# First adaLN columns in groups of 128, the first in-projection weights as single chunks, fewer adaLN tiles on TensorE, gates spread through DRAM, and eight FFN groups in two turns

## Chip, cores and metric

The kernel runs on one core of a Trainium2 chip. The metric is the device time of one execution in microseconds (us), the median of several runs on the chip. The engines are TensorE (PE: matmuls; PEld: its weight loads), VectorE (DVE), ScalarE (ACT), GpSimd (POOL) and SyncE (SP), which issues most DMAs.

## The reference

One decoder block in float32, with 256 tokens of width 2048. A vector c gives six rows of 2048 (shift, scale and gate of two sub-layers) by a product with a 2048 x 12288 matrix, which with 100 MB is the largest tensor. What is computed:

```python
mod = silu(c) @ w_ada + b_ada
sh1, sc1, g1, sh2, sc2, g2 = split(mod, 6)

h = modulate(rms_norm(x, norm1_g), sh1, sc1)        # h * (1 + sc1) + sh1
q, k, v, gb, gc, xt = split(h @ w_in)               # six parts of 1024 columns
attn = moba_attention(rms_norm(q), rms_norm(k), v)  # 8 heads, 256 tokens: one block, causal
conv = gb * causal_dwconv(gc * xt, conv_w, conv_b)  # 3 taps
mixed = concat(rms_norm(attn, attn_out_g), rms_norm(conv, conv_out_g))
x = x + g1 * (mixed @ w_out)

h2 = modulate(rms_norm(x, norm2_g), sh2, sc2)
u = causal_dwconv(h2 @ w_ffn_up, ffn_conv_w, ffn_conv_b)
u_gate, u_up = split(u)                             # 5632 columns each
x = x + g2 * ((silu(u_gate) * u_up) @ w_ffn_down)
```

## The kernel before

**Precision.** Every large product is done in fp32r, in three parts: a weight tile `raw` is split by ScalarE into `hi` (L230, fp32r) and by VectorE into `lo = raw - hi` (L236); the activations are split in the same way. `mm_tok` issues hi·hi, lo·hi and hi·lo (L380, L381, L382) for each chunk of 128 rows and each half of the tokens. In the FFN's first product (called z in the trace) a wide matmul (L673) has both parts of the activations as 512 moving columns, and a low one (L677) multiplies `lo` with 256.

**Slots.** The weight tiles, mostly of 1 MB, form a list of 204 slots in the order in which TensorE works on them: in-projection, out-projection, then the FFN in 22 groups of 256 columns of gate and up, in four segments, each followed by its part of the down-projection. Five `raw` buffers are filled by SyncE in the order in which they will be used; `hi` and `lo` are made two slots ahead (`LA`). All other work is made of small tasks, which tables in `CFG` place at a slot and, within it, before or after the slot's splits. The order of instructions on each engine is written out by this list; no scheduler changes it.

**In-projection.** Its 12 blocks of 512 columns (`q0`, `q1`, `k0` and so on) come in `turns`, each over a range of the 16 chunks of rows, first two chunks of a pair of blocks, later eight of one. Between turns the sums leave PSUM for SBUF (`evac_in`: ScalarE copies `pa_*` at L391, or VectorE adds at L393).

**The adaLN product.** The class `Ada` works on groups of columns, tile by tile (1 MB each). Some groups are done on TensorE with 32 copies of silu(c) as weights (`crep`), four chunks side by side in the array (L286); the others on VectorE, as a product-and-add with a scalar for each partition (L290, L292). A group on TensorE is copied out by `evac` (L303). `cols` turns scale and shift from a row into columns: transposes on TensorE (L319), then a VectorE reduction (L321) or ScalarE copies with a sum (L326). `spread` gives gates to all partitions by a product with 128 columns of ones (L343) and a copy (L344). The first groups hold scale and shift of two chunks, 256 columns each, with two tiles each.

**The start.** x is loaded, normed, and transposed chunk pair by chunk pair (`xn`, L1037, copied at L1040); with the first columns of scale and shift `h_chunks` (L742 to L749) makes the first two chunks of h, and the main loop begins.

**FFN.** The second norm (`norm2`, L541 to L552) makes chunks 0 to 7 of h2 first, and the first four groups (`split`) are multiplied with chunks 0 to 7, then with 8 to 15; the first half's sums wait in SBUF (`up_sum`: ScalarE L587, VectorE L590, and L595 to add both halves). x1, the result of the first sub-layer, stays in SBUF, and its transposes (L496) are made around the end of the out-projection. PSUM's eight banks are one ring (`bank`).

## Time and profile before

| | us |
|---|---|
| median of 3 runs | 1197.08 |
| lowest and highest run | 1196.53, 1200.62 |
| span of the profiled execution | 1195.2 |

The span is the time from the first to the last instruction of one execution under the profiler, and all rows of the trace are measured from its start. The profiled execution has no time of its own beside the span; the median of the runs stands 1.9 us above it.

In rows of the timeline the columns are the start in us, the duration in us, the engine and the line, the operation, output and inputs (partitions x elements), how many instructions the row joins (x), and in brackets the idle time before it and what ended it. The page lists busy time, share of the span and instructions of each engine; a row of the groups gives the total busy time and the mean of one in ns, and the idle time behind the bar. A row of the waits gives the total us, how often, and the longest. `raw`, `hi` and `lo` are the weight tiles, `ada` an adaLN sum, `adac` its columns, `adab` a gate's broadcast, `m` with a letter an in-projection sum, `pa` with a letter that sum in SBUF.

### The profile page before, as it was taken

The page shows a single profiled execution, that of the slowest core. Times are in us where ns is not written, and L with a number is a line of the kernel's source. Part 1 is how long each engine was busy: PE and PEld are TensorE (multiplying, and loading weights), DVE is VectorE, ACT ScalarE, POOL GpSimd, SP SyncE. Part 2 cuts the span into 40 slices and gives each one's busy share as a digit, 9 for nine tenths or more (in the row PEclk, how much of TensorE's full clock was granted, in tenths as well). Part 3 has the DMA queues.
Part 4 walks back from the last instruction along what each step waited for, and adds up shares of the span by engine and source line. Part 5 has one row for each costly group of instructions (what it writes and reads, how often), then busy time and mean ns, then how long its engine had stood idle before and what let it go on. Part 6 is the DMA issues. An engine that isn't in the chain of part 4 may idle for free.

```text
span 1195.2 us, 15484 instructions
## 1 busy us (share of the span) xinstructions
PE 1169.1 (98%) x6041; PEld 962.5 (81%) x6041; DVE 917.4 (77%) x1099; ACT 614.1 (51%) x850; POOL 1.6 (0%) x9
## 2 busy tenths in 40 slices
PE   5999999999999999999999999999999999999998
PEld 3667788877778778888888888888888888888886
DVE  3889989997888988788787587776745667567676
ACT  5654356555766456565645334545434455344452
POOL 0000000000000000000000000000000000000000
PEclk9999999999999999999999999999999999999999
DMA  9999997998869998755777789654565554674543
GB/s 366 357 409 381 369 378 271 386 348 334 293 234 407 345 370 286 240 183 167 247 255 259 263 302 368 210 181 154 186 229 171 197 181 150 217 235 154 175 136 106
DMA packets 194925, 313.78 MB, mean 263 GB/s; under 512 B 6650, under 2 KB 105500, under 8 KB 194596
## 3 DMA queue, kind: packets, MB, share of 16 engines
q1 hardware_dynamic: 194160, 312.52, 74.1%
q8 instruction: 47, 0.77, 0.2%
q10 hardware_dynamic: 692, 0.28, 0.1%
q14 instruction: 26, 0.21, 0.1%
HBM read 310.67 MB, written 2.10 MB: 262 GB/s over the span
## 4 chain that ended last, share of the span: by engine, by line
PE 93%; DVE 3%; DMA 3%; ACT 1%; issue 0%; SPq 0%; ACTq 0%
PE z L673 27%; PE z L677 14%; DMA raw<-in_w_ada_dram 3%; PE ada L286 2%; PE mc L380 1%; PE mc L381 1%; PE mc L382 1%; PE mx L380 1%; PE mq L380 1%; PE mv L382 1%; PE mg L380 1%; PE mk L380 1%; PE mg L382 1%; PE mx L382 1%; PE mg L381 1%; PE mx L381 1%
## 5 line engine op out<-in xcount | busy, mean ns | idle before, releaser
L236 DVE TENSOR_TENSOR lo<-raw,hi 128x2048 fp32r<-128x2048 f32 (+2 forms) x204 | 448.8, 2206 | 167.2 <-ACT hi L230 158.2
L230 ACT ACTIVATE hi<-raw 128x2048 fp32r<-128x2048 f32 (+2 forms) x204 | 375.9, 1848 | 367.2 <-PE z L673 104.5
L673 PE MATMUL z<-h,hi 128*128 128x512 f32 x1408 | 381.3, 395 | 1.1 <-DVE h L573 1.1
L673 PEld LDWEIGHTS z<-h,hi 128*128 128x128 f32 x1408 | 242.2, 189 | 36.7 <-DVE h L573 2.0
L677 PEld LDWEIGHTS z<-h,lo 128*128 128x128 f32 x1408 | 212.6, 189 | 27.8
L677 PE MATMUL z<-h,lo 128*128 128x256 f32 x1408 | 220.3, 281 | 0.0
L292 DVE SCALAR_TENSOR_TENSOR ada<-raw,csil,ada 128x1024 f32<-128x1024 f32 (+2 forms) x165 | 159.5, 968 | 5.8 <-DMA raw<-in_w_ada_dram 1.8
L590 DVE TENSOR_TENSOR ub<-z,ub 128x256 f32<-128x256 f32 x104 | 37.5, 418 | 33.0 <-ACT ub L587 32.8
L604 ACT ACTIVATE uy<-ub,fc,fc 128x256 f32<-128x256 f32 x88 | 45.7, 591 | 5.5 <-DVE uy L611 5.5
L286 PE MATMUL ada<-raw,crep 128*32 128x512 f32 (+1 forms) x320 | 36.5, 566 | 10.2 <-DMA raw<-in_w_ada_dram 10.2
L611 DVE SCALAR_TENSOR_TENSOR uy<-ub,fc,uy 128x254 f32<-128x254 f32 x88 | 42.5, 483 | 3.1
L620 ACT ACTIVATE gh<-uy 128x512 fp32r<-128x512 f32 x22 | 13.9, 632 | 58.1 <-DVE uy L618 58.1
L609 DVE SCALAR_TENSOR_TENSOR uy<-ub,fc,uy 128x255 f32<-128x255 f32 x88 | 42.1, 479 | 1.5 <-ACT uy L604 1.5
L587 ACT ACTIVATE ub<-z 128x256 f32<-128x256 f32 x104 | 32.2, 382 | 11.6 <-PE z L673 11.6
L614 ACT ACTIVATE uy<-uy 128x512 f32<-128x512 f32 x22 | 13.9, 631 | 39.1 <-DVE uy L611 39.1
L286 PEld LDWEIGHTS ada<-raw,crep 128*32 128x32 f32 x320 | 8.4, 113 | 26.4 <-issue 14.3
L621 DVE TENSOR_TENSOR gl<-uy,gh 128x512 fp32r<-128x512 f32 x22 | 15.2, 693 | 15.4 <-ACT gh L620 15.4
L382 PE MATMUL mv<-hi,h 128*128 128x512 f32 x64 | 25.0, 391 | 1.4 <-DVE h L749 1.4
L380 PE MATMUL mc<-hi,h 128*128 128x512 f32 x64 | 26.2, 409 | 0.0
L380 PE MATMUL mk<-hi,h 128*128 128x512 f32 x64 | 25.3, 396 | 0.7 <-ACT h L746 0.7
L380 PE MATMUL mx<-hi,h 128*128 128x512 f32 x64 | 25.8, 402 | 0.0
L380 PE MATMUL mg<-hi,h 128*128 128x512 f32 x64 | 25.5, 398 | 0.0
(541 smaller groups left out, 1854.3 us busy)
## 6 DMA issues: line engine op xcount, KB each, us to landing
raw<-in_w_ada_dram SPq DMA_DIRECT2D x96, 1024.0 KB
raw<-in_w_ffn_up_dram SPq DMA_DIRECT2D x176, 512.0 KB
raw<-in_w_in_dram SPq DMA_DIRECT2D x48, 1024.0 KB
raw<-in_w_ffn_down_dram SPq DMA_DIRECT2D x24, 1024.0 KB
raw<-in_w_ffn_down_dram SPq DMA_DIRECT2D x24, 768.0 KB
raw<-in_w_out_dram SPq DMA_DIRECT2D x16, 1024.0 KB
xr<-in_x_dram SPq DMA_DIRECT2D x2, 1024.0 KB
x<-in_x_dram SPq DMA_DIRECT2D x8, 256.0 KB
```

Of the source, the lines that this page charges most:

```text
L230: act(hi[:, :nk], t[:, :nk], AF.Copy)
L236: V.tensor_tensor(out=lo[:, :nk], in0=t[:, :nk], in1=hi[:, :nk].bitcast(F32), op=ALU.subtract)
L286: mm(self.acc[q:q + 32, :], crep[:, i, :], t[:, j, :], start=(r == 0 and j < 4), stop=(r == self.tiles - 1 and j >= self.rows - 4), tile_p ...
L292: V.scalar_tensor_tensor(out=self.acc, in0=t[:, j, :], scalar=csil[:, i:i + 1], in1=self.acc, op0=ALU.mult, op1=ALU.add)
L380: mm(o, a, hi[:, k], start=(first and k == 0), stop=False)
L382: mm(o, b, hi[:, k], start=False, stop=(last and k == nk - 1))
L590: V.tensor_tensor(out=d, in0=zp[grp][ft][:, :256], in1=d, op=ALU.add)
L604: act(y, b, AF.Identity, bias=fcols[3][:, i:i + 1], scale=fcols[2][:, i:i + 1])
L609: V.scalar_tensor_tensor(out=y[:, 1:], in0=b[:, :255], scalar=fcols[1][:, i:i + 1], in1=y[:, 1:], op0=ALU.mult, op1=ALU.add)
L611: V.scalar_tensor_tensor(out=y[:, 2:], in0=b[:, :254], scalar=fcols[0][:, i:i + 1], in1=y[:, 2:], op0=ALU.mult, op1=ALU.add)
L673: mm(zp[grp][ft], hi[:, j, ft * P:(ft + 1) * P], h2T[k + j], start=k + j == ks[0], stop=k + j == ks[1] - 1)
L677: mm(zp[grp][ft][:, :256], lo[:, j, ft * P:(ft + 1) * P], h2T[k + j][:, :256], start=False, stop=False)
```

## The change

- **First adaLN groups.** Instead of two groups of 256 columns there are four of 128. The first scale and shift (SC_0, SH_0) are done "directly": each weight chunk is the stationary operand and silu(c) the one moving column (16 products each), so that the result stands in a column at once. SC_1 and SH_1 are done as before, but 128 columns wide. Rows of these tiles are 512 bytes long in DRAM.
- **The first weight slots.** The first turn takes three blocks (q0, q1, k0) for chunk 0 alone, the second the same blocks for chunk 1: 768 KB each, loaded and split in three pieces. There are 205 slots.
- **Tiles on TensorE.** 28 rather than 34, and the four tiles of the first groups; VectorE does 8,192 columns rather than 7,936. VectorE's steps are no longer issued when their tile is due, but in numbers given by tables (`pre`, `carry`).
- **Columns.** `cols` has products with one moving column (62 instructions) in place of 64 transposes and of what followed these.
- **Gates.** `spread` makes 32 copies with two products side by side, VectorE adds the bias, ScalarE's queue sends the row to DRAM and later loads it back to all partitions (`broadcast`).
- **FFN.** Eight groups are worked on in two turns. The wide and the low products of a slot are 16 and 16 instead of 4 and 4 by turns. x1 is parked in DRAM and loaded back.
- **Banks.** Each PSUM bank is held (`keep`) and freed (`drop`) by name. A table `move` shifts tasks by slots.

The diff, cut:

```diff
-CFG = {'ada': [[3, 12, 512, False, 51, 12], [3, 0, 512, True, 58, 2], [2, 0, 1024, False, 24, 17],
...
+CFG = {'ada': [[1, 2, 256, True, 1, 4], [0, 2, 256, True, 1, 1], [1, 4, 512, True, 3, 7], [0, 4, 512, False, 2, 7],
...
- 'turns': [['k', 0, 2], ['c', 0, 2], ['g', 0, 2], ['x', 0, 2], ['v', 0, 2], ['q', 0, 2], ['v', 2, 4], ['x', 2, 4],
...
+ 'turns': [['q0', 3, 0, 1], ['q0', 3, 1, 2], ['c0', 2, 0, 2], ['k1', 1, 0, 2], ['g0', 2, 0, 2], ['v0', 2, 0, 2],
...
+ 'pre': {0: 3,
...
+ 'carry': {0: 2,
...
+ 'move': {'att_n 2': (0, 3),
...
- 'split': [4, 8],
+ 'split': [8, 8],
...
-        return ps.tile([P, 512], F32, tag="b", bufs=8, name=name)
+    now, free, live = [0], list(range(8)), {}
+
+    def bank(name, keep=False):
+        i = next(j for j in free if j not in live.values())
+        free.remove(i)
+        free.append(i)
+        t = ps.tile([P, 512], F32, tag=f"b{i}", bufs=1, name=name)
+        if keep:
+            live[id(t)] = i
+        return t
...
+            self.seen += 1
             for j in range(self.rows):
                 i = self.rows * r + j
-                if self.pe:
+                if self.direct:
+                    mm(self.full[:, 0:1], t[:, j, :], csil[:, i:i + 1], start=i == 0, stop=i == NK - 1)
+                elif self.pe:
                     q = 32 * (j % 4)
...
-                elif i == 0:
-                    V.tensor_scalar(self.acc, t[:, j, :], csil[:, i:i + 1], None, op0=ALU.mult)
                 else:
-                    V.scalar_tensor_tensor(out=self.acc, in0=t[:, j, :], scalar=csil[:, i:i + 1],
-                                           in1=self.acc, op0=ALU.mult, op1=ALU.add)
-            load_next()
+                    later.setdefault(self, []).append((t[:, j, :], i, j == self.rows - 1))
...
-                for k in range(n):
-                    nc.tensor.transpose(p[:, k * P:(k + 1) * P], self.acc[:, (h + k) * P:(h + k + 1) * P], ident)
...
+            for k in range(0 if self.direct else m):
+                mm(p[:, k:k + 1], self.acc[:, k * P:(k + 1) * P], (c32 if self.pe else ones)[:, 0:1],
+                   start=True, stop=True)
+            z = p[:, :m]
...
-                mm(p, c32 if self.pe else ones, a, start=True, stop=True)
-                act(a, p, AF.Copy)
-                gB[self.part, self.c0 // 4 + i // 512] = a
...
+            for q in range(a, a + n):
+                mm(p[32 * q:32 * q + 32, :], ones[:, :32], self.acc[:, (q - a) * 512:(q - a + 1) * 512],
+                   start=True, stop=True, tile_position=(0, 32 * q))
...
+                nc.scalar.dma_start(rowsG[self.part, q], gsum[self.part][32 * q:32 * q + 1, :])
...
+        nc.scalar.dma_start(gB[part, f], rowsG[part, f].partition_broadcast(P))
...
+    def park(f):
+        assert f"ev{f}" in done
+        for t in range(2):
+            parked[t, f] = dram.tile([P, 512], F32, name=f"pk{t}{f}")
+            nc.scalar.dma_start(parked[t, f], x1[t, f])
...
-                        for i in range(0, 16, 4):
...
+                        for f in (wide, low) if flip[0] else (low, wide):
+                            for e in order:
+                                f(*e)
...
-    ada_init = [Ada(SC1, 0, 256, True), Ada(SH1, 0, 256, True)]
+    ada_init = [Ada(part, k, P, True) for k in range(2) for part in (SC1, SH1)]
...
+    xn_tr(0)
+    xn_out(0)
+    SC_0.cols()
+    SH_0.consume(0)
+    SH_0.cols()
+    part = pieces(0)
+    part[0]()
+    h_chunks([0])
+    part[1]()
+    part[2]()
+    xn_tr(1, 2)
+    slots[0][2](*splits.pop(0))
...
+        n = sum(len(v) for v in later.values())
+        a = min(n, CFG["pre"].get(i, 1))
+        steps_of(a)
         if more:
             split_lo()
+        steps_of(max(0, n - a - CFG["carry"].get(i, 0)))
```

The order of instructions, at three places. In these rows the engine's line comes first (of the kernel named), then the operation, the output, the inputs and a size. TensorE at the program's start, before: the two tiles of the first scale (`ada_0_138`), of which the trace joins the products, its columns (`adac`), and the first tile of the first shift (`ada_0_199`), with transposes of x (`xn`) between.

```order
L286 MATMUL ada_0_138<-raw,crep 32x256 x16
L172 MATMUL pv_vbc<-ident,vb 128x112
L1037 MATMUL xn_163<-ident,xr 128x128 x4
L319 MATMUL adac_0_173<-ident,adae_0_170 128x128 x2
L1037 MATMUL xn_185<-ident,xr 128x128 x4
L1037 MATMUL xn_192<-ident,xr 128x128 x4
L286 MATMUL ada_0_199<-raw,crep 32x256 x8
L1037 MATMUL xn_210<-ident,xr 128x128 x4
```

Here all eight pairs of x and both groups, each of 256 columns, stand ahead of the first main sum `mk_301`. The same place now: the direct groups (`adad`) stand first, each with one transposition of chunks of x behind it, and the first main sum (`mq_222`).

```order
L514 MATMUL adad_0_146<-csil,raw 128x1 x16
L1388 MATMUL xn_167<-ident,xr 128x128 x4
L514 MATMUL adad_0_177<-csil,raw 128x1 x16
L1388 MATMUL xn_212<-ident,xr 128x128 x4
L1388 MATMUL xn_217<-ident,xr 128x128 x4
L659 MATMUL mq_222<-hi,h_202 128x512
L660 MATMUL mq_222<-lo,h_202 128x512
L661 MATMUL mq_222<-hi,h_202 128x512
L659 MATMUL mq_223<-hi,h_202 128x512
```

Of the eight pairs of x (four transposes each) three now stand ahead of the first main sum, and the other five behind it; the columns need no transposes.

ScalarE behind the first main slots, now; `hi` is a split of a weight tile, `xnT` a copy of transposed x, `pa` an evacuation of a sum.

```order
L1397 ACTIVATE xnT_347<-xn_342 128x512
L1397 ACTIVATE xnT_361<-xn_356 128x512
L453 ACTIVATE hi<-raw 128x2048
L453 ACTIVATE hi<-raw 128x1024
L671 ACTIVATE pa_k_430<-mk_238 128x512
L671 ACTIVATE pa_k_432<-mk_239 128x512
L671 ACTIVATE pa_q_434<-mq_230 128x512
L671 ACTIVATE pa_q_436<-mq_231 128x512
L671 ACTIVATE pa_q_458<-mq_222 128x512
L671 ACTIVATE pa_q_460<-mq_223 128x512
```

Two copies, the splits of the third and the fourth slot and six evacuations stand between the second slot and the third, which needs `hi` and the banks. Before, the copies of x are all issued ahead of the loop, and the same place has:

```order
L230 ACTIVATE hi<-raw 128x2048 x2
L391 ACTIVATE pa_k_353<-mk_301 128x512
L391 ACTIVATE pa_k_355<-mk_302 128x512
L391 ACTIVATE pa_k_357<-mk_315 128x512
L391 ACTIVATE pa_k_359<-mk_316 128x512
L391 ACTIVATE pa_c_393<-mc_365 128x512
L391 ACTIVATE pa_c_395<-mc_366 128x512
```

There the splits of the third and fourth slot stand ahead of the four evacuations of k, with no copy of x in front of them, and the second slot's sums (`pa_c`) follow later.

VectorE in the two-turn part of the FFN, before, where the fourth group's first turn is done (`ub` are half sums, `z` the banks) and the first group's second turn is added:

```order
L590 TENSOR_TENSOR ub_4333<-z_3_4258,ub_4333 128x256
L236 TENSOR_TENSOR lo<-raw,hi 128x2048 x2
L590 TENSOR_TENSOR ub_4424<-z_0_4347,ub_4424 128x256
L590 TENSOR_TENSOR ub_4424<-z_1_4348,ub_4424 128x256
L590 TENSOR_TENSOR ub_4425<-z_2_4349,ub_4425 128x256
L590 TENSOR_TENSOR ub_4425<-z_3_4350,ub_4425 128x256
L595 TENSOR_TENSOR ub_3997<-ub_3997,ub_4424 128x512
```

Now, between the sixth and the seventh group's first turn, with an adaLN tile (`ada_8_3739`) that is worked on between them:

```order
L912 TENSOR_TENSOR ub_4459<-z_3_4372,ub_4459 128x256
L459 TENSOR_TENSOR lo<-raw,hi 128x2048
L530 SCALAR_TENSOR_TENSOR ada_8_3739<-raw,csil,ada_8_3739 128x1024 x2
L566 TENSOR_TENSOR B_95<-adac_12_4516,vbc 128x4
L459 TENSOR_TENSOR lo<-raw,hi 128x2048
L912 TENSOR_TENSOR ub_4559<-z_0_4473,ub_4559 128x256
L912 TENSOR_TENSOR ub_4559<-z_1_4474,ub_4559 128x256
L912 TENSOR_TENSOR ub_4560<-z_2_4475,ub_4560 128x256
L912 TENSOR_TENSOR ub_4560<-z_3_4476,ub_4560 128x256
L459 TENSOR_TENSOR lo<-raw,hi 128x2048
```

The additions of both halves (L917 now) come only after the eighth group.

More of the change, by code (lines that the diff above doesn't have):

```diff
@@ new lines, in tile_block, with flush, steps_of, broadcast @@
+    later = {}
+    gbias, gsum, wideB, rowsG = {}, {}, {}, {}
+    def flush(g):
+        while g in later:
+            g.step()
+    def steps_of(n):
+        for _ in range(n):
+            if later:
+                g = next(iter(later))
+                rest = later.pop(g)
+                later[g] = rest
+                g.step()
+    def broadcast(part, f):
+        if part == G1:
+            gB[part, f] = t2k(f"gB{part}_{f}")
+        else:
+            if f % 2 == 0:
+                wideB[part] = t4k(f"gB{part}_{f}")
+            gB[part, f] = wideB[part][:, (f % 2) * 512:(f % 2) * 512 + 512]
+        nc.scalar.dma_start(gB[part, f], rowsG[part, f].partition_broadcast(P))
@@ L374, in mm_tok @@
         if first:
-            mainp[key] = [bank(f"m{key}{t}") for t in range(2)]
+            mainp[key] = [bank(f"m{key}{t}", keep=True) for t in range(2)]
+        whole[key] = last
         order = [(k, t) for t in range(2) for k in range(nk)] if by_t else [(k, t) for k in range(nk) for t in range(2)]
@@ L382, in mm_tok, with evac_in @@
             mm(o, b, hi[:, k], start=False, stop=(last and k == nk - 1))
-    def evac_in(f):
-        if in_last.get(f) == now[0]:
+    def evac_in(f, last):
+        assert whole.pop(f)
+        if last:
             done.add(f)
@@ L641, in evac_down @@
                 nc.sync.dma_start(out[0, t * P:(t + 1) * P, f * 512:(f + 1) * 512], y)
+            drop(p)
     def gate_down(f):
-        assert f"ed{len(SEGS) - 2}{f}" in done
+        assert all(f"ed{seg}{f}" in done for seg in range(len(SEGS) - 1)) and f"un{f}" in done
         done.add(f"gd{f}")
@@ L717, in tile_block @@
                 at(len(slots), evac_down, seg, f)
+    at(N_OUT + 2, park, 3)
+    for f in range(4):
+        at(len(slots) + CFG["unpark"] + f, unpark, f)
     ready_at = {}
@@ L813, in qk_norm, with after @@
             i = col("k", t, 4 * half)
-            p3 = pacc[f"k{half}", t].rearrange("p (h d) -> p h d", d=HD)
-            V.tensor_tensor(out=p3, in0=p3, in1=rqk[:, i:i + 4].unsqueeze(2).to_broadcast([P, 4, HD]),
-                            op=ALU.mult)
+            for j in range(4):
+                p = pacc[f"k{half}", t][:, j * P:(j + 1) * P]
+                act(p, p, AF.Copy, scale=rqk[:, i + j:i + j + 1])
     att = {}
     ssC = const.tile([P, 2], F32, name="ssC")
+    def after(a, b, h):
+        assert a == "att_t" or f"{a}{h}" in done
+        done.add(f"{b}{h}")
     def att_t(h):
@@ L942, in conv_c @@
     def conv_c(half, h):
+        done.add(f"cc{half}{h}")
         assert f"p{half}" in done
@@ L957, in conv_g @@
     def conv_g(half, h):
+        assert f"cc{half}{h}" in done
         assert f"g{half}" in done
@@ L1055, in tile_block, with pieces, one @@
-    split_hi(slots[1][1])
-    split_lo()
+            if j % 2:
+                V.tensor_copy(xnT[j], xnp[j])
+            else:
+                act(xnT[j], xnp[j], AF.Copy)
+            drop(xnp[j])
+    def pieces(n):
+        t, w = take(), slots[n][1] * 512
+        hi, lo = (sb.tile([P, 4, 512], F32R, tag=tag, bufs=N_HL, name=tag) for tag in ("hi", "lo"))
+        tf, hf, lf = (v.rearrange("p a b -> p (a b)") for v in (t, hi, lo))
+        def one(a):
+            s = slice(a, a + 512)
+            act(hf[:, s], tf[:, s], AF.Copy)
+            V.tensor_tensor(out=lf[:, s], in0=tf[:, s], in1=hf[:, s].bitcast(F32), op=ALU.subtract)
+            if a + 512 == w:
+                splits.append((hi, lo))
+                load_next()
+        return [lambda a=a: one(a) for a in range(0, w, 512)]
@@ new lines, in tile_block @@
+    xn_tr(0)
[10 more added lines that the diff above has]
+    slots[0][2](*splits.pop(0))
+    scale(1024, 2048)
+    xn_out(1, 2)
+    SC_1.consume(0)
+    SC_1.evac()
+    SH_1.consume(0)
+    SC_1.cols()
+    xn_tr(3)
+    SH_1.evac()
+    SH_1.cols()
+    part = pieces(1)
+    part[0]()
+    h_chunks([1])
+    part[1]()
+    part[2]()
+    xn_out(3)
+    slots[1][2](*splits.pop(0))
```

511 lines of the change are left out of this document (396 added, 115 removed), and 22 rows, old and new, of the table CFG.

## The prediction

> **What bounds the kernel now.** I read the page's busy times and chain first, then the waits of TensorE, then the timeline at the places where it waits.
>
> ```profile
> PE 1169.1 (98%) x6041; PEld 962.5 (81%) x6041; DVE 917.4 (77%) x1099; ACT 614.1 (51%) x850; POOL 1.6 (0%) x9
> PE 93%; DVE 3%; DMA 3%; ACT 1%; issue 0%; SPq 0%; ACTq 0%
> PE ada L286 <- DMA raw<-in_w_ada_dram: 10.2, 3, 7.1
> PE n2b L548 <- DVE n2d L546: 1.5, 1, 1.5
> PE mv L382 <- DVE h L749: 1.4, 1, 1.4
> PE z L673 <- DVE h L573: 1.1, 1, 1.1
> 52.40 0.39 PE L382 MATMUL mx<-hi,h 128*128 128x512 f32 x1
> 52.63 0.39 PE L380 MATMUL mx<-hi,h 128*128 128x512 f32 x1
> ```
>
> TensorE is busy 98% of the span of 1195.2 us and makes 93% of the chain that ended last; all its waits for others come to some 22 us, half of them ahead of 35 us. So the time is the sum of what TensorE does, and an edit counts by the TensorE time that it adds or takes, by the start, and by a wait that it makes where TensorE now never waits. The last two rows give the spacing of main matmuls, 52.63 - 52.40 = 0.23 us (0.227 over a long run of such rows): the duration of 0.39 overlaps the next. A slot (one weight tile, 24 of these, or 16 wide and 16 low in the FFN) is about 5.5 us. The sum below is made against the profiled execution; the median of the runs, 1197.08, stands 1.9 above its span.
>
> **The start.** The rows are the second half of x on ScalarE, the four first adaLN tiles, the first main matmul and the wait after the first slot; then a window with the granted clock as the third figure from its end, and two queues of DMA.
>
> ```profile
> 8.49 1.91 ACT L1020 ACTIVATE j<-xr 128x2048 f32<-128x2048 f32 x1 [0.79 <-DMA xr<-in_x_dram]
> 11.26 1.93 PE L286 MATMUL ada<-raw,crep 128*32 128x256 f32 x16 [7.07 <-DMA raw<-in_w_ada_dram]
> 13.90 1.93 PE L286 MATMUL ada<-raw,crep 128*32 128x256 f32 x16 [0.71 <-DMA raw<-in_w_ada_dram]
> 19.27 1.07 PE L286 MATMUL ada<-raw,crep 128*32 128x256 f32 x16
> 21.81 1.07 PE L286 MATMUL ada<-raw,crep 128*32 128x256 f32 x16
> 25.42 0.50 PE L380 MATMUL mk<-hi,h 128*128 128x512 f32 x1 [0.72 <-ACT h L746]
> 30.76 0.39 PE L382 MATMUL mk<-hi,h 128*128 128x512 f32 x1
> 33.53 1.48 PE L286 MATMUL ada<-raw,crep 128*32 128x256 f32 x16 [2.38 <-DMA raw<-in_w_ada_dram]
> 34.93 0.80 PE L380 MATMUL mc<-hi,h 128*128 128x512 f32 x1
> 35.00:40.00 5.00, 5.00 (x18) 4.07 (x18) 3.69 (x5) 4.54 (x6) 0.00 (x0) 0.75 1.03 402
> q1 hardware_dynamic: 194160, 312.52, 74.1%
> q10 hardware_dynamic: 692, 0.28, 0.1%
> ```
>
> The tiles follow each other by 2.64 us (13.90 - 11.26), with one 1 MB weight tile between the second and the third by 5.37: about 2.7 us per MB, the DMA's pace. All begins with what has landed.
>
> Before, rows of the first adaLN tiles are 1024 bytes long; now they are 512. No row shows a 512-byte stream. From the two queues: q1 spends 0.741 x 16 x 1195.2 / 194160 = 73 ns on a packet of 1610 bytes, q10 some 28 ns on one of 405. A line through both gives 32 ns for 512 bytes and 51 for 1024, 1.25 times as much per byte, so 3.3 us per MB. q10's 0.1% is rounded; its bounds of 0.05 and 0.15% make the factor 1.0 to 1.5. I take 1.25.
>
> With x in at 8.5, the landings are then: SC_0 11.9, SH_0 15.3, the first weight slot (768 KB) 17.3, SC_1 20.7, SH_1 24.1, the second slot 26.1, the third 28.8, the fourth (512 KB) 30, and three 256-column tiles 32.7, 35.4, 38.1. TensorE can't do the third slot before the last of those tiles, which stands ahead of it in its order: 38.1 + 1.0 and some five small transposes make 39.6, a lower bound.
>
> SC_0's 16 products with one moving column are fp32, priced below at 0.22; cold, as the tiles above show (1.93 against 1.07), 0.40. The first 12 chunks land at some 11.0, the last 4 at 11.9, and 16 x 0.40 from 11.0 end at 17.4. SH_0's 16 take 3.5, then come B, h on ScalarE and the rest, about 0.8: first main matmul 22.5 (17.5 if the landings alone decide). 18 matmuls take 4.1, to 27. Tiles of SC_1 and SH_1, their evacuation, two products and h: second slot from 30.3 to 34.4.
>
> Now ScalarE sets the pace, since its work for the third slot stands behind h of the second:
>
> ```profile
> 36.62 1.92 ACT L230 ACTIVATE hi<-raw 128x2048 fp32r<-128x2048 f32 x1 [0.46 <-DMA raw<-in_w_in_dram]
> 38.45 2.04 ACT L391 ACTIVATE pa_k<-mk 128x512 f32<-128x512 f32 x4
> 40.35 2.13 ACT L391 ACTIVATE pa_c<-mc 128x512 f32<-128x512 f32 x4
> ```
>
> A split takes 1.83 (38.45 - 36.62), an evacuation (40.35 - 38.45) / 4 = 0.48. The fifth and sixth transposed chunk pairs are copied at about 35.6, then the split of the third slot ends at 37.9 and that of the fourth, half as wide, at 39.0; then the banks are freed one by one, and the third slot's first matmul needs the fifth of these: 41.4. So I take **41.4** for the third slot's start, between 39.6 (DMA alone) and 43.2 (the second slot 1 us later, and all six copies waited for).
>
> From there to the point where 96 main matmuls are done: 24 at 5.5, two products 0.44, 12 at 2.8, two tiles 2.0, two products 0.44, 24 at 5.5: 16.7 us, at 58.1. Before, the 96th is done at 53.40 (below). **+4.7**: the two first slots begin 3 us earlier but are three quarters of a slot each, and what they gain is lost ahead of the third. By then 5 of the tiles on TensorE are done in both.
>
> In before the idle 2.38 us ahead of 33.53 are followed by a clock of 0.75: 18 matmuls in 5 us, where 22 fit at 0.227, so 0.9 us lost. My third slot has 1.8 us of idle ahead of it, and I count no such loss. The Trainium skill ("TensorE: Matmul & The Clock Gate", Part 1, the HAM clock gate) says that an idle window of about 3.4 us halves the clock until a busy window of the same length is over. By that rule a gap of this size should not have cost anything before, while the trace shows a partly reduced clock; an estimate by it for a third slot that finds TensorE cold is 3.4 / 2 = 1.7 us, and the time would be 1199.2 in place of 1197.5.
>
> **TensorE's other work.** The rows are an adaLN tile between main matmuls, four transposes of adaLN columns, products with one moving column, and two gate products.
>
> ```profile
> 53.40 1.07 PE L286 MATMUL ada<-raw,crep 128*32 128x256 f32 x16
> 54.40 0.50 PE L380 MATMUL mv<-hi,h 128*128 128x512 f32 x1
> 60.02 0.38 PE L319 MATMUL adac<-ident,ada 128*128 128x128 f32 x2
> 60.24 0.38 PE L319 MATMUL adac<-ident,adae 128*128 128x128 f32 x2
> 60.38 0.49 PE L380 MATMUL mq<-hi,h 128*128 128x512 f32 x1
> 346.19 0.58 PE L896 MATMUL ssA<-ones,sq 128*128 128x1 f32 x4
> 346.63 0.63 PE L938 MATMUL trc<-ident,pa_c 128*128 128x128 f32 x4
> 703.49 1.88 PE L343 MATMUL adab<-ada,ones 128*128 128x512 f32 x4
> 704.81 0.80 PE L380 MATMUL m('D', 0, 3)0_5868<-hi,gh 128*128 128x512 f32 x1
> 705.45 0.39 PE L381 MATMUL m('D', 0, 3)0_5868<-lo,gh 128*128 128x512 f32 x1
> ```
>
> - Tiles: one takes 54.40 - 53.40 = 1.0. After the start 29 remain before, 23 now: **-6.0**. A fit at all widths: each is 1 MB.
> - Columns: a transpose costs (60.38 - 60.02) / 4 = 0.09, a product with one column (346.63 - 346.19) / 2 = 0.22 (two products, four rows, since fp32 passes twice). Outside the start 60 transposes go, 56 products come: 12.3 - 5.4 = **+6.9**. The low end is the transpose's price, 0.09: 5.0, so -0.4 in all; the high end is half of the row's whole 0.58, 0.29: 16.2, so +10.8.
> - Gates: two products take from 703.49 to 705.45 less one spacing, 1.73; eight 6.9. Now they have 32 columns and go side by side in pairs: between half of it, 3.5, and nothing gained, 6.9; nearest to the adaLN tile, where four lie side by side, I take 4.0: **-2.9**. Bias, DRAM and the broadcast back have some slots of 5.5 us until the gate is read, and the ScalarE queue that issues them is busy half of the time: nothing.
> - The wait of 1.4 at mv: h of the third pair is now made several slots ahead: **-1.4**. What is late next there is the split, which has two slots of lead.
> - The eight transposes of x1 that stood among the first FFN slots' work are done in the wait ahead of z: 8 x 0.09 and their turn, **-0.9**. The wait for n2d I keep.
> - Order of wide and low products in the FFN: the same matmuls at the same spacing: nothing. The x1 parked in DRAM: 4 MB of 314 on queues that are busy 74%: nothing.
>
> Sum: 4.7 - 6.0 + 6.9 - 2.9 - 1.4 - 0.9 = +0.4. Span 1195.6, **time 1197.5**.
>
> **The two-turn FFN groups.** Eight groups instead of four leave half sums in SBUF.
>
> ```profile
> 475.00:498.00 23.00, 23.00 (x134) 20.16 (x133) 20.12 (x27) 12.92 (x24) 0.00 (x0) 1.00 0.62 205
> 474.56 2.29 DVE L236 TENSOR_TENSOR lo<-raw,hi 128x2048 fp32r<-128x2048 f32 x1 [1.32 <-ACT hi L230]
> L590 DVE TENSOR_TENSOR ub<-z,ub 128x256 f32<-128x256 f32 x104 | 37.5, 418 | 33.0 <-ACT ub L587 32.8
> L595 DVE TENSOR_TENSOR ub<-ub,ub 128x512 f32<-128x512 f32 x8 | 5.1, 685 | 0.0
> ```
>
> In that window, where the two-turn groups of before run, VectorE works 20.12 of 23.00 us: 4.9 in a slot of 5.61. The four more groups add 16 adds of 0.418 and 8 of 0.685: 6.7 + 5.5 = 12.2 us, over the 32 slots of the stage 0.4 per slot, so 5.2 to 5.3 in the slots of the stage. It still fits below 5.61, and TensorE is two splits behind VectorE: I count nothing, and from nothing below zero, since no work leaves TensorE there.
>
> **The rivals.**
> - *A, VectorE becomes the bound in that stage.* 5.25 of 5.61 leave 0.36 per slot for waits, and the trace shows waits of 1.32 for the split on ScalarE about every third slot, 0.4 per slot. If each slot comes 0.45 late for 16 slots, it is +7: **1204.5**. It decides once VectorE's waits exceed 0.4 per slot. Against it: part of the waits are due to VectorE being ahead.
> - *B, the products with one column cost what a transpose does.* -7.3 by the prices above: **1190.2**; with the start at the DMA's bound, 1188.4. For it: the row at 346.19 is the only one of its kind, and products that stand alone among wide matmuls may share their latency with these. Against it: it stands among such matmuls too, and gives 0.22.
> - *C, 512-byte rows cost double per byte.* Four tiles of 1 MB at 5.4 instead of 3.3 put 8 us on the landings; the third slot then starts at 47.6 and not 41.4: **1203.7**. Against it: the line through the queues, at most 1.5.
>
> **How the numbers follow.** Forecast 0.50, A 0.17, B 0.23, C 0.10. About 0.5%, 6 us, is what a measurement of this kernel can tell from no change: 1191.1 to 1203.1. The forecast gives 0.46 within and 0.02 on either side; B 0.21 faster and 0.02 within; A 0.13 slower and 0.04 within; C 0.06 and 0.04. That is 0.23, 0.56 and 0.21. The range of 8 in 10 leaves out some of B below and of A and C above: 1189.5 to 1204.5.
>
> **What would show it.** The third slot's first matmul at 41 (39.6 to 43) and what it waits for; a span of 0.22 per one-column product between main matmuls; 1.0 for a pair of gate products; no wait of TensorE for VectorE's split in the two-turn stage; mv's wait gone. A third slot beyond 45, one-column products at 0.1, or waits for lo in most slots of the two-turn stage would prove me wrong.

## The result and the profile after

| | before | changed |
|---|---|---|
| median of 4 runs each, us | 1197.91 | 1208.91 |
| lowest and highest run, us | 1196.53, 1200.62 | 1208.44, 1211.65 |
| span of the profiled execution, us | 1195.2 | 1206.6 |

The changed kernel is slower: its time is 1.0098 of the time before, with a 95% interval of 1.0081 to 1.0116. That is 11.0 us, and 11.4 us in the spans. The forecast was 1197.5, within 1189.5 to 1204.5: it was wrong.

The first fence has two lines of the changed kernel's page (busy times; the chain by engine) and the longer waits of its TensorE (total us, times, longest).

```profile
PE 1180.3 (98%) x6165; PEld 984.7 (82%) x6165; DVE 915.8 (76%) x1085; ACT 610.0 (51%) x813; POOL 12.5 (1%) x30
PE 88%; DMA 5%; DVE 5%; ACT 1%; issue 1%; SPq 0%; ACTq 0%; DVEq 0%
PE pv_vbc L394 <- DMA vb<-in_b_ada_dram: 4.9, 1, 4.9
PE ada L517 <- DMA raw<-in_w_ada_dram: 3.2, 3, 1.8
PE adac L559 <- DVE ub L912: 2.4, 1, 2.4
PE n2b L868 <- DVE n2d L866: 1.4, 1, 1.4
```

TensorE is still busy 98% of the span, and the listed waits are no longer than before. So the page alone doesn't show the loss: TensorE was "busy" for 11 us more (1180.3 against 1169.1) with work that the prediction's sum had priced only 0.4 us longer. The way to the place is to number the main matmuls (in-projection, out-projection, both FFN products: 5408 in either kernel, in the same classes of work) and to compare the starts of the n-th, taken from both traces:

| n | before, us | changed, us | difference |
|---|---|---|---|
| 0 | 25.4 | 27.2 | +1.7 |
| 96 | 54.4 | 71.0 | +16.6 |
| 480 | 155.1 | 174.7 | +19.6 |
| 864 | 245.0 | 264.0 | +18.9 |
| 960 | 277.4 | 291.6 | +14.2 |
| 1440 | 419.6 | 429.5 | +9.9 |
| 1920 | 520.5 | 529.8 | +9.3 |
| 2016 | 537.3 | 553.3 | +16.0 |
| 2880 | 707.0 | 721.3 | +14.3 |
| 3552 | 829.9 | 841.4 | +11.5 |
| 5376 | 1182.7 | 1194.6 | +11.9 |

Two places lose: the start, 16.6 us and another 3 up to the 480th, and the two-turn FFN groups, 6.7 us between the 1920th and the 2016th. From the 480th to the 1920th the changed kernel gains 10 us. Not all of the 16.6 is loss: ahead of the 96th the changed kernel has done ten adaLN tiles and the kernel before six, so 4 us of it are tiles of 1.0 us moved forward, which the forecast's +4.7 holds too. What the start lost against the forecast is 16.6 - 4.7 = 11.9.

**The start.** TensorE's timeline of the changed kernel: both direct groups, matmuls of the first slot, the first of the second slot, and two later waits.

```profile
11.16 6.96 PE L514 MATMUL adad<-csil,raw 128*128 128x1 f32 x32 [1.54 <-DMA raw<-in_w_ada_dram]
18.87 6.83 PE L514 MATMUL adad<-csil,raw 128*128 128x1 f32 x32
27.16 0.78 PE L659 MATMUL mq<-hi,h 128*128 128x512 f32 x1
27.73 0.63 PE L660 MATMUL mq<-lo,h 128*128 128x512 f32 x1
28.16 0.63 PE L661 MATMUL mq<-hi,h 128*128 128x512 f32 x1
32.17 0.39 PE L661 MATMUL mk<-hi,h 128*128 128x512 f32 x1
32.40 0.39 PE L659 MATMUL mk<-hi,h 128*128 128x512 f32 x1
37.35 0.50 PE L659 MATMUL mq<-hi,h 128*128 128x512 f32 x1 [0.89 <-ACT h L1074]
48.78 0.28 PE L394 MATMUL pv_v1c<-ident,v 66*128 66x66 f32 x1 [1.41 <-ACT pa_q L671]
61.79 1.07 PE L517 MATMUL ada<-raw,crep 128*32 128x512 f32 x8 [1.79 <-DMA raw<-in_w_ada_dram]
```

Both groups of 16 products (32 rows, two passes each) take 6.9 us, 0.43 a product; the second was to run at 0.22. The first main matmuls follow at 28.16 - 27.73 = 0.43 us, those at the end of the slot at 0.23: TensorE runs at half its pace from its first instruction to 31 us, although it has worked without a pause since 11.16. Until 24 us the DMA fills the five weight buffers; then it has none free, since the tiles of the slow products still hold theirs (SH_0's until 25.7). Windows of the changed kernel (span in us; busy time of PE, PEld, DVE, ACT, POOL; granted clock; DMA share; GB/s):

```profile
12.00:15.00 3.00, 3.00 (x16) 3.00 (x16) 2.32 (x8) 0.47 (x2) 0.00 (x0) 1.00 1.14 367
18.00:21.00 3.00, 3.00 (x16) 3.00 (x16) 0.32 (x2) 1.11 (x2) 0.00 (x0) 1.00 1.14 346
24.00:27.00 3.00, 3.00 (x15) 3.00 (x16) 1.16 (x4) 1.01 (x2) 0.00 (x0) 1.00 0.26 64
33.00:36.00 3.00, 2.75 (x71) 2.29 (x70) 0.32 (x2) 1.07 (x3) 0.00 (x0) 1.00 0.18 48
```

The kernel before, in the second of these windows:

```profile
18.00:21.00 3.00, 2.97 (x33) 2.22 (x34) 1.68 (x4) 2.78 (x4) 0.00 (x0) 1.00 1.09 387
```

In the changed kernel the DMA share falls to 0.26 and 0.18. At 61.79, and again at 70.04 (1.06 us), TensorE waits for a tile. That the pause makes these waits is not shown: runs below that start earlier have waits at the same tiles. (The column of the granted clock reads 1.00 in the first window, though only 16 rows of one-column products are done there in 3 us; more on that at the end.)

**The two-turn stage.** In the changed kernel: the wait of TensorE, ScalarE's split ahead of it, and the window behind it.

```profile
537.87 1.05 PE L559 MATMUL adac<-ones,ada 128*128 128x1 f32 x8 [2.39 <-DVE ub L912]
532.04 1.92 ACT L453 ACTIVATE hi<-raw 128x2048 fp32r<-128x2048 f32 x1 [7.91 <-DMA raw<-in_w_ffn_up_dram]
540.00:545.00 5.00, 5.00 (x22) 4.44 (x22) 4.96 (x5) 2.66 (x3) 0.00 (x0) 0.71 1.07 371
```

ScalarE has waited 7.91 us for weights; TensorE then waits 2.39 us, and with that pause its clock falls to 0.71 in the next window, which costs 5 x 0.29 = 1.5 us more.

### The profile page after: what moved, and what is told of

Same layout as the page of the kernel before. It is cut to its first block, busy times and chain, and to the rows that moved or that the text cites. A ratio compares the mean times of both kernels' runs of the same rounds, so it can differ in the third digit from the quotient of the medians.

```text
span 1206.6 us, 15789 instructions
## 1 busy us (share of the span) xinstructions
PE 1180.3 (98%) x6165; PEld 984.7 (82%) x6165; DVE 915.8 (76%) x1085; ACT 610.0 (51%) x813; POOL 12.5 (1%) x30
## 4 chain that ended last, share of the span: by engine, by line
PE 88%; DMA 5%; DVE 5%; ACT 1%; issue 1%; SPq 0%; ACTq 0%; DVEq 0%
PE z L996 23%; PE z L1000 12%; DMA raw<-in_w_ada_dram 2%; DVE lo L459 2%; DMA raw<-in_w_ffn_up_dram 2%; PE ada L517 2%; DVE ada L530 1%; PE mq L659 1%; PE mq L661 1%; PE mx L659 1%; PE mq L660 1%; PE mx L661 1%; PE mx L660 1%; DMA raw<-in_w_in_dram 1%; PE adad L514 1%; ACT hi L453 1%
## 5 line engine op out<-in xcount | busy, mean ns | idle before, releaser
L996 PE MATMUL z<-h,hi 128*128 128x512 f32 x1408 | 329.1, 390 | 0.1
L996 PEld LDWEIGHTS z<-h,hi 128*128 128x128 f32 x1408 | 261.9, 188 | 52.8 <-PE x1t L816 0.3
L1000 PEld LDWEIGHTS z<-h,lo 128*128 128x128 f32 x1408 | 175.9, 193 | 3.5
L1000 PE MATMUL z<-h,lo 128*128 128x256 f32 x1408 | 177.4, 284 | 0.0
L530 DVE SCALAR_TENSOR_TENSOR ada<-raw,csil,ada 128x1024 f32<-128x1024 f32 (+1 forms) x135 | 156.1, 1161 | 1.8 <-DMA raw<-in_w_ada_dram 0.4
L912 DVE TENSOR_TENSOR ub<-z,ub 128x256 f32<-128x256 f32 x120 | 42.7, 415 | 37.4 <-ACT ub L909 37.3
L909 ACT ACTIVATE ub<-z 128x256 f32<-128x256 f32 x120 | 38.0, 381 | 19.6 <-PE z L996 19.5
L517 PE MATMUL ada<-raw,crep 128*32 128x512 f32 (+2 forms) x320 | 30.8, 493 | 3.3 <-DMA raw<-in_w_ada_dram 3.2
L659 PE MATMUL mq<-hi,h 128*128 128x512 f32 x64 | 26.1, 408 | 0.9 <-ACT h L1074 0.9
L659 PE MATMUL mx<-hi,h 128*128 128x512 f32 x64 | 25.7, 402 | 0.0
L661 PE MATMUL mq<-hi,h 128*128 128x512 f32 x64 | 25.6, 400 | 0.1
L660 PE MATMUL mq<-lo,h 128*128 128x512 f32 x64 | 25.6, 401 | 0.0
```

What stands on the lines that cost most here:

```text
L517: mm(self.acc[q:q + 32, :], crep[:, i, :], t[:, j, :], start=(r == 0 and j < 4), stop=(r == self.tiles - 1 and j >= self.rows - 4), tile_p ...
L530: V.scalar_tensor_tensor(out=self.acc, in0=t, scalar=csil[:, i:i + 1], in1=self.acc, op0=ALU.mult, op1=ALU.add)
L659: mm(o, a, hi[:, k], start=(first and k == 0), stop=False)
L660: mm(o, a, lo[:, k], start=False, stop=False)
L661: mm(o, b, hi[:, k], start=False, stop=(last and k == nk - 1))
L912: V.tensor_tensor(out=d, in0=zp[grp][ft][:, :256], in1=d, op=ALU.add)
```

## The experiments

In the diffs, only the lines that tell one kernel from the other.

### Is it the one-column products? The first groups with copies

Against the changed kernel:

```diff
-            self.direct = n == P and c0 == 0
+            self.direct = False
...
+    SC_0.evac()
     SC_0.cols()
     SH_0.consume(0)
+    SH_0.evac()
     SH_0.cols()
```

> The changed kernel with the first two groups done like the next two (32 copies of silu(c) as weights, 128 columns moving, then evacuated and turned by one product) instead of by 16 one-column products each. Theory 'cold products': the 64 rows of the direct groups took 13.5 us because TensorE is cold and stays cold in them (0.43 us a product where 0.22 was priced), they hold the weight buffers and with them the DMA queue; without them the first main matmul comes at 19 to 21 instead of 27.2, the third slot's first by 44 instead of 50.3, and the time is 1198 to 1203. Rival 'landings and ScalarE': 512-byte rows and the splits and evacuations behind the second slot set the third slot's start; then the first main matmul comes earlier but the third slot stays at 48 to 50, and the time is 1206 or more.

Measured: 1203.65 us (1.0046 of before, 1.0031 to 1.0060), some 5 us less than the changed kernel. The first main matmul comes at 20.9, 6.2 earlier, the third slot at 44.0 and the 96th matmul at 66.0, still 5.0 earlier. The first theory's numbers hold for the start of the matmuls and for the third slot, and its time is missed by little; the products are a part of the loss, not the whole. TensorE is cold with the copies too: its main matmuls follow each other by 0.43 us until 24.5. What is saved is that a group's 16 copies, at that pace, take 1.9 us where 16 one-column products took 6.9. The profiled execution took 1206.54 us, 2.9 above the median, and in it the lead is down to 0.3 us at the 960th matmul. Where it goes, three views of it show: TensorE behind the first slot, later ScalarE and TensorE near 280 us, and the window there.

```profile
27.14 1.96 PE L517 MATMUL ada<-raw,crep 128*32 128x128 f32 x64
31.31 0.50 PE L659 MATMUL mq<-hi,h 128*128 128x512 f32 x1 [0.89 <-ACT h L1074]
274.04 1.93 ACT L453 ACTIVATE hi<-raw 128x2048 fp32r<-128x2048 f32 x1 [3.78 <-DMA raw<-in_w_in_dram]
280.99 0.80 PE L1173 MATMUL as<-kT,qT 128*128 128x128 f32 x2 [1.01 <-ACT kT L1166]
280.00:285.00 5.00, 4.01 (x12) 3.32 (x13) 4.93 (x7) 3.42 (x6) 0.00 (x0) 0.66 0.60 179
```

The second slot begins 4.2 us after the first has ended (27.14): two tiles, their evacuation, columns and h stand between two slots of 4 us each. And at 274 ScalarE waits 3.78 us for weights; at 281 TensorE waits for ScalarE, and its clock falls to 0.66 for the next 5 us. TensorE is 4 us earlier there and the weights are not. That holds for this execution; in the medians the 5 us stay.

### Are they slow by themselves, or cold? TensorE warmed before them

```diff
+    heat = bank("heat")
+    for i in range(16):
+        mm(heat[:, :P], ones, ones, start=True, stop=True)
     vbc = to_cols(vb, nb, "vbc")
+    for i in range(6):
+        mm(heat[:, :P], ones, ones, start=True, stop=True)
```

> The changed kernel with 22 products of ones by ones (128 columns, result unused) on TensorE while it waits for the first data, from about 4.3 us to 11 us. Theory 'cold products, warmable': once warm, the one-column products keep the clock, take 0.22 us each, the first main matmul comes at 20 to 22 and the time is 1199 to 1203. Rival 'one-column products do not count as work': they start at 0.22 and go back to 0.43 within a few us, or are 0.43 throughout, and the time is 1206 or more. Second rival, 'their price is 0.43 whatever the clock': the main matmuls of the first slot run at 0.227 from the start while the products still take 0.43.

Measured: 1206.11 us (1.0071, 1.0044 to 1.0098), the first main matmul at 23.6. TensorE's timeline of this run, and two of its windows:

```profile
4.18 5.95 PE L1365 MATMUL heat<-ones 128*128 128x128 f32 x32
11.41 3.63 PE L514 MATMUL adad<-csil,raw 128*128 128x1 f32 x32
15.37 6.75 PE L514 MATMUL adad<-csil,raw 128*128 128x1 f32 x32
13.00:15.00 2.00, 2.00 (x20) 2.00 (x20) 1.70 (x5) 0.00 (x0) 0.00 (x0) 1.00 1.13 373
17.00:19.00 2.00, 2.00 (x12) 2.00 (x11) 0.00 (x0) 0.00 (x0) 0.00 (x0) 0.50 1.16 352
```

Warm, the first 16 products take 3.63 us, 0.23 each, as priced; after some 4 us of nothing but such products and four transposes, the second 16 take 6.75 us at a granted clock of 0.50, although TensorE hasn't paused. So the price of 0.22 is right and depends on the clock, and one-column products don't keep the clock up: the first rival, in its first form. The second rival (0.43 whatever the clock) falls. The first theory's time, 1199 to 1203, is missed as well.

### What does the whole start cost? The old start in the changed kernel

```diff
- 'turns': [['q0', 3, 0, 1], ['q0', 3, 1, 2], ['c0', 2, 0, 2], ['k1', 1, 0, 2], ['g0', 2, 0, 2], ['v0', 2, 0, 2],
+ 'turns': [['q0', 2, 0, 2], ['k0', 1, 0, 2], ['c0', 2, 0, 2], ['k1', 1, 0, 2], ['g0', 2, 0, 2], ['v0', 2, 0, 2],
...
-    ada_init = [Ada(part, k, P, True) for k in range(2) for part in (SC1, SH1)]
+    ada_init = [Ada(SC1, 0, 256, True), Ada(SH1, 0, 256, True)]
...
+    xn_cols(0)
+    SC.evac()
+    SC.cols()
+    split_hi(slots[0][1])
+    split_lo()
+    xn_cols(1, 2)
+    SH.consume(0)
+    xn_cols(3, 4, 5)
+    SH.consume(1)
+    SH.evac()
+    SH.cols()
+    h_chunks(range(2))
+    xn_cols(6, 7)
+    split_hi(slots[1][1])
+    split_lo()
```

> The changed kernel with the start of the kernel before: first scale and shift in two groups of 256 columns, first slots of two chunks (q0 and q1, then k0), all of x transposed ahead of the loop; everything behind is as changed. Theory 'the start makes the loss': the 96th main matmul comes at 54 to 57 and not at 71, and since the changed rest gains 11 us and loses 6.7 in the two-turn stage, the time is 1191 to 1197. Rival 'weights decide until 290 us': the DMA queues and VectorE are full in the in-projection, so that the 14 to 16 us gained at the 96th matmul shrink to under 8 at the 960th, and the time is 1200 to 1205. Third: without the changed start the moved tasks no longer fit and it is over 1206.

Measured: 1197.06 us (1.0002, 0.9984 to 1.0020): 11.9 us less than the changed kernel, at the upper edge of what was expected. The start makes the loss; the rest of the change neither gains nor loses on balance, although the two-turn stage still loses in it. The rival falls: against the changed kernel the profiled execution (1203.35, 6.3 above the median) is 6.7 us earlier at the 96th matmul and 7.1 at the 960th, and that of the next run, which has the same start, 11.4 and 11.5, so what is gained at the start is kept. The expectation for the 96th matmul (54 to 57) was missed: 64.3 in this run, 59.6 in the next. Of the 5.2 us that 59.6 lies behind the kernel before, 4 are the tiles moved forward. Of the 4.7 between the two runs, 1.5 are there at the first main matmul (29.1 and 27.6); the windows show the others. The first two rows are of this run, the third of the next one.

```profile
48.00:54.00 6.00, 3.62 (x31) 1.55 (x29) 4.19 (x4) 4.90 (x8) 0.00 (x0) 0.92 1.06 396
54.00:60.00 6.00, 6.00 (x21) 4.30 (x15) 2.59 (x7) 1.99 (x2) 0.00 (x0) 0.51 1.01 393
```

```profile
54.00:60.00 6.00, 5.72 (x30) 3.73 (x29) 3.04 (x3) 2.88 (x3) 0.00 (x0) 1.00 1.03 410
```

In this run TensorE pauses for 0.75 and 1.63 us ahead of 53, with one tile between, in the next for 0.39 and 1.64 ahead of 51.2; the clock is halved for 6 us in the one and not in the other. That alone is worth some 3 us (21 rows against 30), and the runs of this kernel spread from 1192.9 to 1204.0.

### The two-turn stage: the deferred steps

In the changed kernel, in slots 66 to 85:

```diff
-        a = min(n, CFG["pre"].get(i, 1))
+        a = n if 66 <= i < 86 else min(n, CFG["pre"].get(i, 1))
```

> The changed kernel, in which VectorE does all adaLN steps that are due ahead of each split in slots 66 to 85, none deferred by the tables. Theory 'held buffers': in the two-turn stage deferred steps hold two of the five raw buffers while VectorE waits for a split whose weights can't be loaded for want of a buffer; then the loss of 6.7 us between the 1920th and the 2016th main matmul against the kernel before falls below 2, and the time is 1202 to 1205. Rival 'VectorE is full': the lo split then comes still later behind the steps, the loss stays at 5 or grows, 1207 or more. Second rival 'DMA is full': the stage asks for more bytes than the queues give; the loss stays at 5 to 7, and the DMA share there stays above 1.0 for 25 us.

Measured: 1205.65 us (1.0064, 1.0046 to 1.0082), 3.3 less than the changed kernel. Between the 1920th and the 2016th matmul the loss is 2.5 us instead of 6.7. It isn't below 2, but what is left is no stall: 12 one-column products stand there, which in the kernel before stand elsewhere. The first fence has these products in this run. The second is the changed kernel by contrast: VectorE and ScalarE some 40 us ahead of its stall, and a window 20 us ahead of it.

```profile
536.08 0.95 PE L559 MATMUL adac<-ones,ada 128*128 128x1 f32 x8
542.54 1.84 PE L559 MATMUL adac<-ones,ada 128*128 128x1 f32 x16
```

```profile
494.79 2.29 DVE L459 TENSOR_TENSOR lo<-raw,hi 128x2048 fp32r<-128x2048 f32 x1 [4.32 <-ACT hi L453]
497.00 5.37 DVE L530 SCALAR_TENSOR_TENSOR ada<-raw,csil,ada 128x1024 f32<-128x1024 f32 x6
492.83 1.92 ACT L453 ACTIVATE hi<-raw 128x2048 fp32r<-128x2048 f32 x1 [5.11 <-DMA raw<-in_w_ffn_up_dram]
510.00:520.00 10.00, 10.00 (x60) 8.92 (x60) 6.47 (x9) 4.93 (x6) 0.00 (x0) 1.00 0.77 267
```

TensorE waits for nothing, and the 24 rows are 0.95 + 1.84 = 2.8 us of work. In the changed kernel VectorE stands idle for 4.32 us, waiting for a split for whose weights ScalarE has waited 5.11, and does six adaLN steps only then; until they are done, their tiles hold buffers. With the steps done earlier TensorE's stall is gone, as the theory of held buffers has it. VectorE being full is not it, since more work ahead of the splits made the stage faster, nor is it the second rival, a full DMA: the loss did not stay, and from 510 to 520, ahead of the stall, the DMA is busy for 0.77 of the time.

Both together, the old start and no deferral:

> As the run with the old start, and VectorE does all adaLN steps that are due ahead of each split in slots 66 to 85. If both causes stand by themselves, 3 us less than that run: 1188 to 1194, faster than the kernel before. If the two-turn stage loses because TensorE is early or late against the weights, rather than by the deferred steps, the difference is under 1 us.

Measured: 1194.82 us (0.9976, 0.9965 to 0.9987): faster than the kernel before by 3.0 us, though 0.8 above the expected window, and 2.2 less than with the old start alone, where 3 were expected. The intervals of these two runs overlap a little, so the traces have to decide: from the 1920th to the 2016th matmul the run with the old start takes 25.2 us, this one 19.4, as in the run without deferral alone. Each cause stands by itself.

### Eight groups in two turns, alone

In the kernel before, `'split': [4, 8]` becomes `[8, 8]`, nothing else.

> The kernel before with eight FFN groups in two turns instead of four, nothing else. If the additional copies and adds (16 copies, 16 adds of 0.42 us, 8 of 0.69) cost nothing, as forecast: 1196 to 1200. If they make VectorE the bound in that stage (the rival A of the prediction): 1201 to 1206. In that kernel the adaLN groups for the second half of h2 are loaded some 8 slots earlier than in the changed one, so a loss here would be the turns' own, and no loss would leave the adaLN tiles of that stage as the cause.

Measured: 1216.20 us (1.0153, 1.0134 to 1.0172): worse than either theory. The 1440th to the 2304th matmul come when they came before; the loss arises in the second turns (3.0 at the 2400th, 18.4 at the 2688th). The waits of TensorE in this run:

```profile
PE z L677 <- DVE lo L236: 5.9, 2, 3.1
PE m('D', 0, 0)0_5611 L381 <- DVE lo L236: 5.4, 2, 3.9
```

TensorE waits for VectorE's split. In the second turn a group takes two slots, 11.2 us, in which VectorE has its convolution, its gate, the adds of both halves and two splits, and in this kernel also adaLN steps of the second gate. So these were loaded later, from slots 100 and 120 on:

```diff
-         [5, 0, 1024, False, 86, 25], [4, 8, 512, False, 46, 13], [0, 2, 256, False, 0, 7], [1, 2, 256, True, 0, 6],
+         [5, 0, 1024, False, 100, 20], [4, 8, 512, False, 46, 13], [0, 2, 256, False, 0, 7], [1, 2, 256, True, 0, 6],
...
-         [0, 12, 512, False, 15, 9], [4, 12, 512, False, 60, 10], [5, 8, 1024, False, 107, 10]],
+         [0, 12, 512, False, 15, 9], [4, 12, 512, False, 60, 10], [5, 8, 1024, False, 120, 10]],
```

> The kernel before with eight FFN groups in two turns, and the two adaLN groups of the second gate (16 tiles on VectorE) loaded from slots 100 and 120 on instead of 86 and 107. The eight groups alone cost 18 us, all of it where their second turns run (slots 80 to 95): VectorE has 15.1 us of work for the 11.2 us of a group's two slots, 2.6 of it adaLN steps. Theory 'VectorE is full in the second turns': without these steps 12.5 us remain, the loss falls to 3 to 10 us, 1201 to 1208. Rival 'the gate and convolution of a group can't be made in two slots in that order of tasks': the loss stays above 14, over 1211.

Measured: 1210.86 us (1.0099, 1.0079 to 1.0118), above the expected 1201 to 1208, since the later load makes a wait of its own: 2.9 us for the gate, which with the halved clock behind it and the gate's own products, moved there, are 6.5 us ahead of the 3552nd matmul. In the second turns themselves the loss is 9.2 at the 2688th matmul in place of 18.4, within the 3 to 10 that went with VectorE being full. Half of the loss is the adaLN steps; the other half stays in this order of tasks. VectorE's additions of both halves, once for each group, show it: in this run, then in the changed kernel.

```profile
610.33 1.28 DVE L595 TENSOR_TENSOR ub<-ub,ub 128x512 f32<-128x512 f32 x2
622.97 1.28 DVE L595 TENSOR_TENSOR ub<-ub,ub 128x512 f32<-128x512 f32 x2
```

```profile
622.26 1.28 DVE L917 TENSOR_TENSOR ub<-ub,ub 128x512 f32<-128x512 f32 x2
632.84 1.28 DVE L917 TENSOR_TENSOR ub<-ub,ub 128x512 f32<-128x512 f32 x2
```

Without adaLN steps VectorE still needs 622.97 - 610.33 = 12.6 us for a group, more than TensorE's 11.2. The changed kernel has no loss there (16.0 at the 2016th, 15.0 at the 2592nd matmul): it loads the second gate from slot 123 on and moves the gates of groups 3 to 8 up to five slots later, and a group whose gate was moved away takes VectorE 632.84 - 622.26 = 10.6 us. What the later gates alone are worth in the time wasn't tried.

### The order of wide and low products

In the kernel before:

```diff
-                        for i in range(0, 16, 4):
-                            four = order[i:i + 4]
...
+                        for f in (wide, low) if flip[0] else (low, wide):
+                            for e in order:
+                                f(*e)
```

> The kernel before with the changed order of the FFN's first product alone: 16 wide and 16 low matmuls by turns instead of 4 and 4. The prediction counted nothing for it. Theory 'fewer changes of width': in stretches without waits the changed kernel gains 0.16 us on each 96 matmuls of that product against the kernel before; over 2816 of them that is 4.7 us, so 1191.5 to 1193.5. Rival 'it costs nothing', as forecast: the gain comes from something else in the changed kernel, 1196 to 1198.

Measured: 1192.63 us (0.9965, 0.9953 to 0.9977). TensorE's timeline of the kernel before, then of this run (z by fours, then by the slot):

```profile
560.24 1.09 PE L673 MATMUL z<-h,hi 128*128 128x512 f32 x4
561.17 0.63 PE L677 MATMUL z<-h,lo 128*128 128x256 f32 x4
561.64 1.09 PE L673 MATMUL z<-h,hi 128*128 128x512 f32 x4
```

```profile
561.07 7.44 PE L674 MATMUL z<-h,hi 128*128 128x512 f32 x32
568.35 2.92 PE L678 MATMUL z<-h,lo 128*128 128x256 f32 x23
```

Four wide matmuls take 561.17 - 560.24 = 0.93 us, 0.2325 each; 32 in a row 568.35 - 561.07 = 7.28, 0.2275 each. On the mean of all 1408, the wide ones go from 0.2323 to 0.2277 us from start to start, which is 6.4 us, and the low ones from 0.1187 to 0.1201, 2.1 us in return: 4.3 us by the rows, 5.2 by the medians. What the order does in the array no row shows; the gain is measured.

### A version that beats both

The kernel before with that order, and with the gates of the changed kernel (32 copies, two products side by side, a row through DRAM):

```diff
-                mm(p, c32 if self.pe else ones, a, start=True, stop=True)
-                act(a, p, AF.Copy)
...
+                mm(p[q:q + 32, :], (c32 if self.pe else ones)[:, :32], self.acc[:, i:i + 512], start=True, stop=True,
+                   tile_position=(0, q))
...
+                nc.scalar.dma_start(gB[self.part, f], rowsG[self.part, f].partition_broadcast(P))
```

> The kernel before with the 16/16 order (1192.6 in its own run), and gates as in the changed kernel: 32 copies with two products side by side, one row sent to DRAM and loaded back to all partitions one slot later. By the rows of both traces the eight products take 3.9 us in place of 6.1 to 6.9: 2.2 to 3.0 us less, so 1189.5 to 1191. If the round trip through DRAM makes an evacuation wait for its gate, 1193 or more.

Measured: 1191.41 us (0.9943, 0.9930 to 0.9957), just above the expected window; the gates give 1.2 us against the run with the order alone, less than the 2.2 to 3.0 expected, and as the intervals of the two runs overlap, not clear of noise. It is 6.3 us faster than the kernel before, and its median lies 17.5 below that of the changed one.

## Why the prediction was wrong, step by step

- *What bounds:* right. TensorE's work, its clock and the start set the time. (Of TensorE's waits before, 16 of 21 us lie ahead of 35 us, not half.)
- *The start, +4.7:* wrong, +16.6. The step that failed first is "SH_0's 16 take 3.5": they took 6.83. The price of 0.22 is right for a warm TensorE; that TensorE would be warm after 16 such products was taken for granted, and no row that the prediction shows carries it. From there each step came later: the first main matmul 27.2 instead of 22.5; the first slot's 18 matmuls, of which half ran cold, 6.0 us instead of 4.1; the second slot 37.4 instead of 30.3; the third 50.1 instead of 41.4. That is 8.7 us; in the run with copies the third slot starts at 44.0, so 6.1 of them go with the cold one-column products.
- *From the third slot to the 96th matmul:* too short. The 96 were done at 69.0, 18.9 us behind the third slot's start instead of 16.7, 1.8 of it the wait at 61.79; another 1.1 is waited ahead of the tile before the next matmul. The prediction reckoned this part from TensorE's work alone, and it let the loads follow each other without asking for a free buffer: its last 256-column tile of the first three was to land at 38.1, while SyncE issued the loads of these three from 34.3 on. The run with copies, which starts earlier, waits 1.1, 1.6 and 1.0 us for tiles in the same stretch, so the cold products are not the only cause of such waits, and which share they have stays open. 8.7 + 2.2 + 1.1 make 12.0, the 11.9 above. The run with copies shows the products' share of the whole (5.0 us at the 96th matmul, 5.3 in the time), the runs with the old start all of it (11.4 us at the 96th matmul in the second of them, 11.9 in the time of the first).
- *The clock after a pause:* the prediction counted nothing for it. TensorE had no pause between 11 and 27 us and was cold all the same, so the question it weighed (a pause ahead of the third slot) was not the one that mattered. Pauses did cost, though: 2.39 us of idle time in the two-turn stage were followed by a clock of 0.71. The Trainium skill ("TensorE: Matmul & The Clock Gate", Part 1) ties the clock to how busy the array was in a window of about 3.4 us; the warmed run agrees with such a window (3.6 us of one-column products and four transposes, then half clock), and by that rule a stream of these counts as idle.
- *Tiles, columns, gates:* the sizes were near. Eight one-column products take 1.84 us in the row at 542.54 of the run without deferral (0.23 each, 0.22 forecast). A gate's two products, read as the prediction read them (to the second row behind, less its spacing), take 1.0 to 1.1 us now: 4.2 for four pairs (forecast 4.0), where before they took 6.9, so -2.6 for -2.9. The 6.1 in the expectation of the last version counts to the next row alone, but there the next row (704.81, 0.80 us long) overlaps the last gate row.
- *mv's wait:* gone, as forecast. *z's wait for h:* gone; *n2d's* stays, 1.4.
- *Order of wide and low, nothing:* wrong, -4.7 by the numbered matmuls of the changed kernel, -5.2 by the medians of the run with that order alone. The prediction put it at nothing because the matmuls are the same; their spacing is not (0.2323 and 0.2277 for a wide one).
- *The two-turn stage, nothing:* wrong. 6.7 are lost there, 2.8 of it priced column products that moved there, and about 4 a stall with the clock's fall behind it. Rival A gave 7 us for this stage and named VectorE as the bound; the price is near, the mechanism is not: VectorE stood idle (4.3 us, some 40 us ahead of the stall), and its deferred steps held the weight buffers. In the kernel before, with eight groups alone, VectorE does become the bound, but in the second turns.
- *Rival B* (cheap column products) and *C* (512-byte rows at double cost) fell. A one-column product takes 0.23 us. In the window from 18 to 21 us, where the trace has only 512-byte rows, the DMA moves 346 GB/s; in the same window the kernel before, with 1024-byte rows, moves 387. That is 1.12 times as much time per byte, where the prediction took 1.25 and the rival 2.

The sum closes: +0.4 as forecast, 11.9 more at the start, some 4 of stall, and -4.7 for the order give +11.6; the spans differ by 11.4. That it closes to 0.2 is in part luck, since the stall and the order's share are known to half a microsecond at best.

## What to carry to other kernels

A price taken from a row holds for the clock under which it was taken: ask of each new first instruction on TensorE whether it will find the clock up, and whether it keeps it up. Where a ring of a few buffers feeds everything, whoever holds a buffer longer (a slow first product, a deferred step) stops the loads for all, and the bill comes slots later on another engine. And when a change is a bundle, number the main instructions and compare their times: here that told in one table that most of the bundle gained and two parts of it lost.
